# Depthwise-convolution module on one core: tap seeds in PSUM, the products of a tile in strict order, fillers in the middle of a block, and another division of the layer norm's additions

## The chip, the cores and the metric

The kernel runs on one core of one Trainium2 chip. The metric is the device time of that core in microseconds (us). A run of this kernel takes 2839.5 us (the median of three, from 2835.58 to 2844.86).

## What is computed

One inference step of a two-layer decoder for 1040 prompt columns (1024 tokens and 16 learned ones) and 32 sample columns. The change lies in the convolution module of layer 0, and in the cache work that runs in its shadow:

```
def conv_module(x, prefix, w_pw1, b_pw1, w_dw, b_dw, ln_g, ln_b, w_pw2, b_pw2):
    a, g = jnp.split(x @ w_pw1 + b_pw1, 2, axis=-1)
    u = a * jax.nn.sigmoid(g)
    y, tail = causal_dwconv(u, prefix, w_dw)          # 31 taps for each of 1024 channels
    y = jax.nn.silu(layer_norm(y + b_dw, ln_g, ln_b))
    return y @ w_pw2 + b_pw2, tail
```

The cache work is a key norm: for each of 128 cached pages the latents are multiplied by w_uk (16 heads of 64 columns), and the sum of squares of each head is kept. Layer 1 needs these sums much later.

## The kernel before

Activations lie with channels on the 128 partitions and 1074 columns (T0) along the free axis, in eight tiles of channels (KD). Each fp32 factor is split into a rounded high part and a low remainder (`split`: the high part by ScalarE, the difference by VectorE, or by GpSimd where `self.help` is set), and a product is three matmuls (`wh`, `wl` are weights, `xh`, `xl` activations).

The convolution module has four stages. First, the input's RMS norm. Second, a loop over eight tiles c: two products (value `a` and gate `g`, PSUM tiles `g`) in three thirds of 358 columns each, with 48 matmuls to a third (line 395), then `glu`: ScalarE's sigmoid (`sg`, line 378) and VectorE's product into `u` (line 379). `u` holds even and odd columns apart. Then `conv31` makes 31 taps out of three shorter filters on the even part, the odd part and their sum `fb` (line 477): `p0` with 16 taps, `p1` with 15 and `p2` with 16. ScalarE writes the first tap of each (the seed, line 481) into SBUF, and VectorE adds the others one by one in a PSUM accumulator `a` (line 488); the instruction for tap 1 reads the seed. GpSimd multiplies the ends of the filters (`ra`, line 484) and the sample columns (`p`, line 502), which VectorE sums (lines 486 and 504). ScalarE copies the state columns into `us` (lines 407, 408). Loop tiles overlap: the products of tile c run beside the taps of tile c-1.

Third, the layer norm: TensorE sums the eight tiles with a matrix of ones (line 529), VectorE subtracts the mean (line 537), ScalarE squares (543), VectorE and GpSimd add the squares (546, 549, 551), TensorE sums them over channels (287), VectorE takes the inverse root, copies it out to rows (`rx`, 264), TensorE transposes these (266) and ScalarE copies them to `rstd` (268); then each tile is scaled (426), goes through silu (428) and is split. Fourth, the second product with `pw2` (line 171; the first two of its eight tiles of outputs run side by side), and the residual (448).

The cache work is a Python generator: each `next(self.fill)` writes one group, three matmuls of 512 columns (line 603, here called a filler) and its sums of squares. By its place among the eight of a page group, the sums go to ScalarE alone (one 512-column group is eight squares of 64 columns with an accumulator, line 615), to a square (606) with a reduction by VectorE (611), or with halvings by GpSimd ahead of that (610). The constants say after how many matmuls a filler is written, and which places go to which engine: there are 256 in all, 16 and 30 ahead of the loop, 24 in each of tiles 1 to 7, then 12 and 11 among the matmuls of the mean (`FILL1`, `FILL0`), 15 behind them (`FILL2`) and 4 behind the splits (`NLN`). That uses up all 256.

The order on each engine is that of a scheduler which follows priorities and its own model of time; inside `with self.manual()` TensorE keeps the order written.

## Time and profile before

| | |
|---|---|
| median of three runs | 2839.5 us |
| profiled execution | 2836.05 us, of which the span is 2834.3 us |
| granted TensorE clock, mean | 0.966 of full speed |
| loop over tiles 1 to 6 | 129 to 396 us, 44.5 us a tile |
| last tile's convolution and mean | 403 to 455 us |
| layer norm up to the first matmul of the second product | 455 to 495 us |
| second product | 495 to 604 us |

Busy time on an engine says how long instructions ran there, not how long it held others up. On TensorE the rows overlap a little, since one matmul begins before the row of the last has ended. Stretches below are cut by hand at the places where the loop repeats.

### The profile page before, as it was taken

Reading aid. Unit: us, or ns where it says so; the run is one execution under the profiler, and the core shown is the slowest. Engines: PE = TensorE matmul, PEld = TensorE weight load, DVE = VectorE, ACT = ScalarE, POOL = GpSimd, SP = SyncE. Lnnn points to the kernel's source line nnn. Section 1 sums busy time; section 2 is a strip of 40 time slices with the busy share of each in tenths; the row PEclk is TensorE's granted clock in tenths of the full one; section 3 lists DMA queues with packets and bytes.
Section 4 is the critical chain, followed back from the end, with each engine's and each line's share of the span. In section 5 each row is a group of like instructions: output and inputs, shape, how many; then the busy total and the mean of one; then the engine's idle time right before and its main releaser. Section 6 shows DMA issues by size and latency. Waiting matters only on the chain.

```text
span 2834.3 us, 47489 instructions
## 1 busy us (share of the span) xinstructions
PE 2675.1 (94%) x16916; PEld 2456.8 (87%) x16916; DVE 1911.5 (67%) x3521; ACT 1380.9 (49%) x4074; POOL 665.5 (23%) x923
## 2 busy tenths in 40 slices
PE   7999986999999999999799999988999999999999
PEld 5888864999999999999667676656999999999999
DVE  8899997569888874234776767565358777766131
ACT  6778778435554553023555564555335544544010
POOL 1457542005333330001201212100005333321000
PEclk9999997999999999999889999978999999999999
DMA  4111110412322236122100001257502222227122
GB/s 136 55 39 57 40 48 20 153 47 76 101 80 91 85 115 225 40 93 90 37 10 26 23 16 42 73 168 225 183 33 76 72 86 78 79 86 257 45 85 74
DMA packets 127778, 238.30 MB, mean 84 GB/s; under 512 B 39779, under 2 KB 81141, under 8 KB 127413
## 3 DMA queue, kind: packets, MB, share of 16 engines
q1 hardware_dynamic: 103828, 200.82, 22.1%
q0 software_dynamic: 9600, 32.36, 3.1%
q10 hardware_dynamic: 14112, 2.09, 0.4%
q8 instruction: 133, 2.18, 0.3%
q14 instruction: 105, 0.85, 0.1%
HBM read 183.90 MB, written 51.31 MB: 83 GB/s over the span
## 4 chain that ended last, share of the span: by engine, by line
PE 80%; DVE 7%; ACT 6%; DMA 2%; issue 2%; SPq 2%; POOL 0%; ACTq 0%; DVEq 0%
PE ps L742 29%; PE ps L171 22%; PE v L1280 5%; PE pk L603 4%; PE ps L791 3%; PE g L395 3%; PE p L147 2%; DVE a L488 2%; PE ps L193 2%; ACT qq L615 2%; PE ps L960 1%; PE p L1290 1%; PE s L1250 1%; PE p L1292 1%; PE p L1293 1%
## 5 line engine op out<-in xcount | busy, mean ns | idle before, releaser
L135 ACT ACTIVATE wh<-raw 128x512 fp32r<-128x512 f32 (+2 forms) x256 | 191.3, 750 | 566.3 <-PE ps L171 360.0
L136 DVE TENSOR_TENSOR wl<-raw,wh 128x512 fp32r<-128x512 f32 (+2 forms) x244 | 201.1, 828 | 104.9 <-ACT wh L135 102.8
L888 DVE TENSOR_TENSOR x<-ps,x 128x1074 f32<-128x1074 f32 (+1 forms) x48 | 60.9, 1270 | 289.5 <-PE ps L171 289.4
L712 DVE SCALAR_TENSOR_TENSOR c<-ub,c,c 128x1040 f32<-128x1040 f32 (+1 forms) x176 | 225.2, 1312 | 30.1 <-ACT c L709 29.3
L615 ACT ACTIVATE qq<-pk 128x64 f32<-128x64 f32 x936 | 198.2, 248 | 76.8 <-PE pk L603 76.2
L615 ACT ACTIVATION_READ_ACCUMULATOR qq<-pk 128x1 f32 x936 | 194.3, 232 | 0.1
L1280 PE MATMUL v<-pf,vf 128*128 128x512 f32 (+4 forms) x448 | 180.2, 486 | 11.8 <-ACT pf L1297 11.5
L707 POOL COPY sb<-ub 128x32 f32<-128x32 f32 x88 | 88.4, 1006 | 398.1 <-DVE ub L753 359.6
L610 POOL TENSOR_TENSOR sq<-sq 128x256 f32<-128x256 f32 x198 | 130.1, 659 | 181.7 <-ACT sq L606 174.4
L603 PE MATMUL pk<-ukh,ch 128*128 128x512 f32 x256 | 115.2, 451 | 47.2 <-ACT qq L615 17.1
L1297 ACT ACTIVATE pf<-p 128x512 f32<-128x512 f32 (+4 forms) x224 | 99.5, 450 | 122.9 <-DVE p L1295 102.2
L171 PE MATMUL ps<-xh,wh 128*128 128x358 f32 (+1 forms) x672 | 147.8, 328 | 2.6 <-DVE x L888 1.6
L171 PE MATMUL ps<-xh,wl 128*128 128x358 f32 (+1 forms) x672 | 147.3, 327 | 0.4 <-DVE wl L136 0.4
L171 PE MATMUL ps<-al,wh 128*128 128x358 f32 (+1 forms) x672 | 147.2, 327 | 0.0
L171 PE MATMUL ps<-xl,wh 128*128 128x358 f32 (+1 forms) x672 | 146.8, 326 | 0.0
L171 PE MATMUL ps<-ah,wl 128*128 128x358 f32 (+1 forms) x672 | 146.5, 326 | 0.0
L171 PE MATMUL ps<-ah,wh 128*128 128x358 f32 (+1 forms) x672 | 146.2, 326 | 0.0
L488 DVE SCALAR_TENSOR_TENSOR a<-u,c,a 128x512 f32<-128x512 f32 x200 | 137.8, 742 | 0.0
L709 ACT ACTIVATE c<-ub,c 128x1074 f32<-128x1074 f32 (+1 forms) x88 | 101.3, 1185 | 67.3 <-DVE ub L753 53.1
L395 PE MATMUL g<-xh,wh 128*128 128x358 f32 x336 | 111.1, 331 | 18.0 <-DVE u L379 16.2
L171 PEld LDWEIGHTS ps<-xh,wh 128*128 128x128 f32 x672 | 116.2, 190 | 4.8 <-ACT ah L135 2.2
L135 ACT ACTIVATE wh<-s 128x512 fp32r<-128x512 f32 x120 | 75.5, 630 | 87.8 <-PE ps L742 81.2
(585 smaller groups left out, 9116.2 us busy)
## 6 DMA issues: line engine op xcount, KB each, us to landing
raw<-wup SPq DMA_DIRECT2D x88, 512.0 KB, 3.5
pg<-ctn SPq DMA_DIRECT2D x128, 192.0 KB, 2.6
raw<-wdn SPq DMA_DIRECT2D x32, 448.0 KB, 3.4
raw<-pw SPq DMA_DIRECT2D x24, 512.0 KB, 3.7
d_a<-c POOLq DMA_DIRECT2D x22, 537.0 KB, 3.5
raw<-d_a SPq DMA_DIRECT2D x22, 537.0 KB, 4.9
d_a<-c POOLq DMA_DIRECT2D x22, 531.0 KB, 3.1
raw<-d_a SPq DMA_DIRECT2D x22, 531.0 KB, 5.5
```

The costliest lines, as they stand in the source:

```text
L135: return (nc.scalar.activation(h, src, AF.Copy), (eng or nc.vector).tensor_tensor(out=l, in0=src, in1=h.bitcast(F32), op=ALU.subtract))
L136: (eng or nc.vector).tensor_tensor(out=l, in0=src, in1=h.bitcast(F32), op=ALU.subtract))
L171: nc.tensor.matmul(p[:, c, :ch], s[:, k * 128:(k + 1) * 128], m[k][:, off + c * ch:off + (c + 1) * ch], start=k == 0 and i == 0, stop=k == ...
L395: nc.tensor.matmul(p[:, 0], x[:, k * 128:(k + 1) * 128], m[k][:, t * ch:t * ch + ch], start=k == 0 and i == 0, stop=k == KD - 1 and i == 2)
L488: nc.vector.scalar_tensor_tensor(out=p[:, :ND] if j == n - 1 else acc, in0=x[:, j:j + ND], scalar=w[:, j:j + 1], in1=p[:, :ND] if j == 1 e ...
L603: nc.tensor.matmul(ps, s[:, j, :], m[:, 512 * c:512 * c + 512], start=i == 0, stop=i == 2)
L610: nc.gpsimd.tensor_tensor(out=v[:, :, :n], in0=v[:, :, :n], in1=v[:, :, n:2 * n], op=ALU.add)
L615: nc.scalar.activation(q, ps[:, 64 * h:64 * h + 64], AF.Square, accum_out=ss[:, p, 8 * c + h:8 * c + h + 1])
L709: x = nc.scalar.activation(c, ub, AF.Copy, scale=wd[:, t, 2:3])
L712: nc.vector.scalar_tensor_tensor(out=c[:, 2:pe], in0=ub[:, tap:tap + pe - 2], scalar=wd[:, t, tap:tap + 1], in1=c[:, 2:pe], op0=ALU.mult, ...
L742: nc.tensor.matmul(ps, w[:, s], m[:, lo:hi], start=first and k == 0 and i == 0, stop=k == KD // 2 - 1 and i == 2, skip_group_check=True)
L1280: nc.tensor.matmul(o[:, at_:], vf[:m, b, c], p[:m, :512 - at_], start=b == 0, stop=last)
```

## The change

Seven edits. (1) The seeds of `p0` and `p1` are written by ScalarE into the PSUM accumulator, so that tap 1 reads PSUM; the order of the two filters is turned, and `p2`, whose seed stays in SBUF, uses the accumulator of `p1`. (2) GpSimd's products `ra` and `p` wait for the addition `fb` (`after`). (3) The state copies go from ScalarE to GpSimd. (4) Each third's matmuls stand behind all of the third before (`self.wedge`), and a filler is written after three matmuls of each six. (5) `self.help` stays on in the last tile and through the mean, so that GpSimd makes the differences of cache latents there. (6) Among the matmuls of the mean there are 12 and 9 fillers, whose odd places go to GpSimd alone (it halves 64 to 1). None stand behind them in the layer norm; the 21 that are left are written into the second product, 8 into the first two tiles of outputs (`EVERY3`), the others one after each nine matmuls (`EVERY2`), with the sums on VectorE. (7) The squares are added in two heaps, 0 to 2 on GpSimd and 3 to 7 on VectorE, and TensorE sums both heaps in one accumulation (`add_rows`).

```diff
-FILL0 = 11
+FILL0 = 9
 FILL1 = 2
-FILL2 = 15
-NLN = 4
+FILL2 = 0
+NLN = 0
+EVERY3 = 18
...
-ONPL0 = ()
-ONPL1 = (0, 3, 6)
+ONPL0 = (1, 3, 5, 7)
+ONPL1 = range(8)
+HEADS = (0, 3)
...
+    def after(self, late, early):
+        why = mybir.DependencyInfo(mybir.DependencyClass.Sync, mybir.DependencyReason.DATA)
+        self.tc.add_manual_dep(late.ins, early.ins.name, why, reason="order")
...
+    def add_rows(self, t, qs, tn):
+        with self.manual():
+            for k, q in enumerate(qs):
+                for b in range(NB):
+                    lo = min(128 * b, tn - 128)
+                    self.nc.tensor.matmul(t[:, 2 * b:2 * b + 2], q[:, lo:lo + 128], self.ones[:, 0:2], start=k == 0 and b == 0,
+                                          stop=k == len(qs) - 1 and b == NB - 1, skip_group_check=True)
...
-                self.help = 0 < c < KD - 1
+                self.help = c > 0
...
-                                        nc.tensor.matmul(p[:, 0], x[:, k * 128:(k + 1) * 128], m[k][:, t * ch:t * ch + ch],
-                                                         start=k == 0 and i == 0, stop=k == KD - 1 and i == 2)
+                                        y = nc.tensor.matmul(p[:, 0], x[:, k * 128:(k + 1) * 128], m[k][:, t * ch:t * ch + ch],
+                                                             start=k == 0 and i == 0, stop=k == KD - 1 and i == 2)
+                                        self.follow(y, self.wedge)
+                                        self.wedge = []
                                         cnt += 1
-                                        if EVERY and cnt % EVERY == 0:
+                                        if EVERY and cnt % EVERY == EVERY // 2:
                                             next(self.fill, None)
+                        self.wedge = [y]
                         glu(*ps, t)
...
-                    nc.scalar.activation(us[:, 0:30].rearrange("p (b e) -> p b e", e=2), u[:, :, 520:535].rearrange("p e b -> p b e"), AF.Copy)
+                    nc.gpsimd.tensor_copy(us[:, 0:30].rearrange("p (b e) -> p b e", e=2), u[:, :, 520:535].rearrange("p e b -> p b e"))
...
-            self.on_dve, self.on_pool = ONLN, ONPL1
             self.groups(NLN)
             self.on_dve, self.on_pool = range(8), ONPL2
...
-                ahead = self.gemms(ahead, hh, ll, 0, T0, EVERY2)
+                ahead = self.gemms(ahead, hh, ll, 0, T0, EVERY3)
...
-        nc.vector.tensor_tensor(out=s, in0=u[:, 1, 0:535], in1=u[:, 0, 1:536], op=ALU.add)
-        def taps(p, x, w, n, name):
+        first = nc.vector.tensor_tensor(out=s, in0=u[:, 1, 0:535], in1=u[:, 0, 1:536], op=ALU.add)
+        def taps(p, x, w, n, name, seed=True):
             m = p.shape[1]
             acc = self.pa.tile([128, 512], F32, name=name)[:, :ND]
-            nc.scalar.activation(p[:, :ND], x[:, 0:ND], AF.Copy, scale=w[:, 0:1])
+            to = acc if seed else p[:, :ND]
+            nc.scalar.activation(to, x[:, 0:ND], AF.Copy, scale=w[:, 0:1])
...
-                                               in1=p[:, :ND] if j == 1 else acc, op0=ALU.mult, op1=ALU.add)
+                                               in1=to if j == 1 else acc, op0=ALU.mult, op1=ALU.add)
...
-        for _ in zip_longest(taps(p0, u[:, 0], w31[:, c, 0::2], 16, "a0"), taps(p1, u[:, 1], w31[:, c, 1::2], 15, "a1")):
+        for _ in zip_longest(taps(p1, u[:, 1], w31[:, c, 1::2], 15, "a1"), taps(p0, u[:, 0], w31[:, c, 0::2], 16, "a0")):
             pass
-        for _ in taps(p2, s, wsum[:, c], 16, "a0"):
+        for _ in taps(p2, s, wsum[:, c], 16, "a1", False):
...
-        self.on_dve = ONLN0
-        self.on_pool = ONPL0
+        self.on_dve, self.on_pool, self.halve = (), ONPL0, 1
...
+        sums = self.pp.tile([128, 3, 512], F32, name="ps")
+        t = sums[:, 2, 400:400 + 2 * NB]
...
+            qs = []
             for k in range(KD):
-                if k == 0:
-                    self.sq_add(sq, ys[k], 0, T0)
-                    continue
                 q = self.xpool(k).tile([128, self.tw], F32R, name=f"xl{k}").bitcast(F32)
                 nc.scalar.activation(q, ys[k], AF.Square)
-                if k in ONPOOL:
...
+                if k in HEADS:
+                    qs.append(q)
                 else:
-                    nc.vector.tensor_tensor(out=sq[:, :T0], in0=sq[:, :T0], in1=q, op=ALU.add)
-                if k == ADDAT:
-                    nc.vector.tensor_tensor(out=sq[:, :T0], in0=sq[:, :T0], in1=odd, op=ALU.add)
+                    (nc.gpsimd if len(qs) == 1 else nc.vector).tensor_tensor(out=qs[-1], in0=qs[-1], in1=q, op=ALU.add)
+            self.add_rows(t, qs, T0)
         self.groups(FILL2)
```

Three places show how the instructions move.

VectorE at the border of two tiles, before: `u` of the last third, the end of the old tile, and the start of the new one (`a_3389` and `a_3395` are the new tile's accumulators, `fa` holds the seeds).

```order
L379 SCALAR_TENSOR_TENSOR u<-g,c_58,sg 128x179x2
L488 SCALAR_TENSOR_TENSOR fb<-fb,wsum,a_2674 128x512
L498 TENSOR_TENSOR x_2631<-fb,fa 128x520
L409 MEMSET u 128x1
L477 TENSOR_TENSOR fb<-u 128x535
L486 TENSOR_REDUCE fa<-ra_3397 128x8
L488 SCALAR_TENSOR_TENSOR a_3389<-u,c_58,fa 128x512
L488 SCALAR_TENSOR_TENSOR a_3395<-u,c_58,fa 128x512
L488 SCALAR_TENSOR_TENSOR a_3389<-u,c_58,a_3389 128x512
L488 SCALAR_TENSOR_TENSOR a_3395<-u,c_58,a_3395 128x512
```

The same place with the change (`a_3392` and `a_3398` are the new tile's accumulators).

```order
L507 SCALAR_TENSOR_TENSOR fb<-fb,wsum,a_2677 128x512
L517 TENSOR_TENSOR x_2634<-fb,fa 128x520
L393 SCALAR_TENSOR_TENSOR u<-g,c_58,sg 128x179x2
L507 SCALAR_TENSOR_TENSOR a_3392<-u,c_58,a_3392 128x512
L507 SCALAR_TENSOR_TENSOR a_3398<-u,c_58,a_3398 128x512
L507 SCALAR_TENSOR_TENSOR a_3392<-u,c_58,a_3392 128x512
L427 MEMSET u 128x1
L626 TENSOR_REDUCE ss<-sq 128x8
L507 SCALAR_TENSOR_TENSOR a_3398<-u,c_58,a_3398 128x512
L495 TENSOR_TENSOR fb<-u 128x535
L507 SCALAR_TENSOR_TENSOR a_3392<-u,c_58,a_3392 128x512
```

The old tile now ends ahead of `u`, the first taps stand right behind `u`, the addition `fb` comes after four of them, and the reductions of `ra` after that.

GpSimd at the same border, before: from the last difference of weights to the first reuse of the squares.

```order
L136 TENSOR_TENSOR wl<-raw,wh 128x1024
L484 TENSOR_TENSOR ra_2643<-u,c_58 128x8x15
L610 TENSOR_TENSOR sq<-sq 128x8x32
L502 TENSOR_TENSOR p<-us,c_58 128x992
L484 TENSOR_TENSOR ra_2637<-u,c_58 128x144
L610 TENSOR_TENSOR sq<-sq 128x8x16
L136 TENSOR_TENSOR cl<-ct,ch 128x512
```

The same place with the change.

```order
L134 TENSOR_TENSOR wl<-raw,wh 128x1024
L624 TENSOR_TENSOR sq<-sq 128x8x32
L425 COPY us<-u 128x30
L426 COPY us<-u 128x32
L624 TENSOR_TENSOR sq<-sq 128x8x16
L134 TENSOR_TENSOR cl<-ct,ch 128x512
L624 TENSOR_TENSOR sq<-sq 128x8x32
L624 TENSOR_TENSOR sq<-sq 128x8x16
L503 TENSOR_TENSOR ra_2640<-u,c_58 128x8x15
L503 TENSOR_TENSOR ra_2646<-u,c_58 128x144
L521 TENSOR_TENSOR p<-us,c_58 128x992
```

Two copies and a difference `cl` (the latter stood behind the products before) now stand between `u` and the products.

VectorE in the layer norm, before: from the last mean subtraction to the inverse root (`sq` is the heap, `xl` are squares, `cl` and `ss` belong to fillers).

```order
L537 SCALAR_TENSOR_TENSOR x_6401<-ps,x_6401 128x1074
L611 TENSOR_REDUCE ss<-sq 128x8
L549 TENSOR_TENSOR sq<-sq,xl_7129 128x1074
L136 TENSOR_TENSOR cl<-ct,ch 128x512
L549 TENSOR_TENSOR sq<-sq,xl_7135 128x1074
L549 TENSOR_TENSOR sq<-sq,xl_7141 128x1074
L611 TENSOR_REDUCE ss<-sq 128x8
L549 TENSOR_TENSOR sq<-sq,xl_7144 128x1074
L551 TENSOR_TENSOR sq<-sq,xl_7127 128x1074
L611 TENSOR_REDUCE ss<-sq 128x8 x2
L251 TENSOR_SCALAR nr_v<-ps 128x9
```

The same place with the change.

```order
L554 SCALAR_TENSOR_TENSOR x_6404<-ps,x_6404 128x1074
L562 TENSOR_TENSOR xl_7016<-xl_7016,xl_7018 128x1074
L562 TENSOR_TENSOR xl_7016<-xl_7016,xl_7021 128x1074
L562 TENSOR_TENSOR xl_7016<-xl_7016,xl_7024 128x1074
L562 TENSOR_TENSOR xl_7016<-xl_7016,xl_7027 128x1074
L253 TENSOR_SCALAR nr_v<-ps 128x9
```

The fillers' rows are gone from between the additions, and four additions are left.

## Rows read from the trace of the kernel before

**Rows 1.** The page: its first line, and busy time, share of the span and number of instructions of each engine over the whole span.

```profile
span 2834.3 us, 47489 instructions
...
PE 2675.1 (94%) x16916; PEld 2456.8 (87%) x16916; DVE 1911.5 (67%) x3521; ACT 1380.9 (49%) x4074; POOL 665.5 (23%) x923
```

**Rows 2.** Busy time by stretch. Columns: the stretch, its length, busy time (and number of instructions) of PE, PEld, DVE, ACT and POOL, then the granted TensorE clock, the DMA share and GB/s. One tile in the middle of the loop, the last tile's convolution, the layer norm, and the first of the second product.

```profile
218.00:262.50 44.50, 41.31 (x218) 37.03 (x217) 43.01 (x71) 33.97 (x218) 28.94 (x34) 1.00 0.17 48
410.00:455.00 45.00, 33.73 (x103) 20.00 (x101) 36.96 (x57) 39.20 (x358) 0.60 (x2) 0.89 0.08 25
455.00:495.00 40.00, 24.86 (x77) 15.19 (x75) 29.51 (x39) 30.29 (x156) 15.42 (x14) 0.68 0.05 14
495.00:500.00 5.00, 5.00 (x16) 4.71 (x17) 5.00 (x5) 5.00 (x10) 0.00 (x0) 0.50 0.00 0
```

**Rows 3.** Waits from 129 to 396 us, which are six of the eight tiles. Columns: who waited for whom, us in total, times, longest.

```profile
PE g L395 <- DVE u L379: 16.2, 6, 3.0
...
DVE u L379 <- ACT sg L378: 5.1, 6, 1.2
```

**Rows 4.** VectorE's groups of instructions in the same six tiles. Columns: line, engine, operation, output and inputs with shapes, count, busy us, mean ns, idle time ahead of them.

```profile
L488 DVE SCALAR_TENSOR_TENSOR a<-u,c,a 128x512 f32<-128x512 f32 x150 | 103.8, 741 | 0.0
...
L488 DVE SCALAR_TENSOR_TENSOR a<-u,c,fa 128x512 f32<-128x512 f32 x12 | 26.6, 2259 | 0.0
```

**Rows 5.** VectorE in order of time, in tile 0, in a middle tile (with one row of GpSimd, POOL), and in the last tile. Columns: start, us (of all xN together), line, operation, output and inputs, count, and in brackets the idle time ahead and what ended it.

```profile
87.92 2.59 DVE L477 TENSOR_TENSOR fb<-u 128x535 f32<-128x535 f32 x1
...
226.09 0.84 DVE L477 TENSOR_TENSOR fb<-u 128x535 f32<-128x535 f32 x1
...
227.03 4.40 DVE L488 SCALAR_TENSOR_TENSOR a<-u,c,fa 128x512 f32<-128x512 f32 x2
...
227.48 3.40 POOL L502 TENSOR_TENSOR p<-us,c 128x992 f32<-128x992 f32 x1
...
405.36 2.69 DVE L477 TENSOR_TENSOR fb<-u 128x535 f32<-128x535 f32 x1
...
413.18 1.41 DVE L488 SCALAR_TENSOR_TENSOR a<-u,c,fa 128x512 f32<-128x512 f32 x2
...
430.92 0.69 DVE L136 TENSOR_TENSOR cl<-ct,ch 128x512 fp32r<-128x512 f32 x1 [2.56 <-ACT ch L135]
...
445.19 0.69 DVE L136 TENSOR_TENSOR cl<-ct,ch 128x512 fp32r<-128x512 f32 x1 [1.56 <-ACT ch L135]
```

**Rows 6.** GpSimd's groups in the six tiles, shapes apart (columns as in the group of VectorE).

```profile
L610 POOL TENSOR_TENSOR sq<-sq 128x256 f32<-128x256 f32 x71 | 56.8, 800 | 59.4 <-ACT sq L606 59.2
...
L610 POOL TENSOR_TENSOR sq<-sq 128x128 f32<-128x128 f32 x72 | 33.9, 471 | 5.2
...
L136 POOL TENSOR_TENSOR cl<-ct,ch 128x512 fp32r<-128x512 f32 x15 | 19.4, 1292 | 27.3 <-ACT ch L135 27.3
```

**Rows 7.** ScalarE: the two tap seeds of a tile, 80 to 400 us.

```profile
L481 ACT ACTIVATE fa<-u,c 128x512 f32<-128x512 f32 x14 | 9.4, 724 | 0.8 <-DVE u L409 0.3
```

**Rows 8.** GpSimd over the whole span: the two nearest forms to a small strided copy.

```profile
L707 POOL COPY sb<-ub 128x32 f32<-128x32 f32 x88 | 88.4, 1006 | 398.1 <-DVE ub L753 359.6 <-ACT ub L800 38.4
...
L1107 POOL COPY rnew<-rrk 64x4 f32<-64x4 f32 x4 | 0.8, 210 | 23.4 <-DVE rrk L256 23.4
```

**Rows 9.** The chain that ended last, in order of time (start, us, what): a block of six products and a filler in a tile, then from the last row of the layer norm into the second product.

```profile
243.20 0.69 PE pk L603 x3
243.88 0.99 PE g L395 x6
...
488.54 0.32 ACT rstd L268
...
492.76 1.17 ACT x L428
...
493.93 0.99 ACT xh L135
...
494.97 1.26 PE ps L171 x3
...
496.23 1.28 PE pk L603 x3
...
507.95 0.70 PE pk L603 x3
```

**Rows 10.** VectorE in order of time through the layer norm (columns as in the earlier timeline).

```profile
451.32 0.70 DVE L498 TENSOR_TENSOR x<-fb,fa 128x520 f32<-128x520 f32 x1
...
455.25 9.56 DVE L537 SCALAR_TENSOR_TENSOR x<-ps,x 128x1074 f32<-128x1074 f32 x8 [3.23 <-PE ps L529]
...
474.79 1.42 DVE L551 TENSOR_TENSOR sq<-sq,xl 128x1074 f32<-128x1074 f32 x1
...
480.30 0.17 DVE L251 TENSOR_SCALAR nr_v<-ps 128x9 f32<-128x9 f32 x1 [3.31 <-PE ps L287]
...
482.55 1.47 DVE L264 COPY rx<-r 128x384 f32<-128x384 f32 x3
...
488.89 3.65 DVE L426 TENSOR_TENSOR x<-x,rstd 128x1074 f32<-128x1074 f32 x3 [0.52 <-ACT rstd L268]
```

**Rows 11.** One addition of a row of squares: on VectorE outside the layer norm, and on GpSimd in it.

```profile
L279 DVE TENSOR_TENSOR sq<-sq,q 128x1074 f32<-128x1074 f32 x12 | 15.6, 1300 | 6.1 <-ACT q L278 5.9
...
L546 POOL TENSOR_TENSOR xl<-xl,xl 128x1074 f32<-128x1074 f32 x2 | 5.4, 2704 | 3.2 <-ACT xl L543 3.2
```

More of the change, by code (lines that the diff above doesn't have):

```diff
@@ L266, in spread @@
                 nc.tensor.transpose(ps[:, c, b * 128:(b + 1) * 128], rx[:, 3 * c + b, :], self.cst("ident"))
-            w = min(384, tn - 384 * c)
+            w, n = min(384, 128 * (NB - 1) - 384 * c), min(0, tn - 384 * c - 384)
             nc.scalar.activation(out[:, 384 * c:384 * c + w], ps[:, c, :w], AF.Copy)
+            if n:
+                nc.scalar.activation(out[:, 384 * c + w:tn], ps[:, c, w - n:384], AF.Copy)
     def sq_add(self, sq, x, k, tn):
@@ L272, in sq_add @@
         if k == 0:
-            if sq.shape[1] > T0:
-                nc.gpsimd.memset(sq[:, tn:], 0.0)
             nc.scalar.activation(sq[:, :tn], x, AF.Square)
@@ L289, in token_rstd, with rows_rstd @@
         return r9, ps
-    def rows_rstd(self, sq, tn):
-        r9, ps = self.token_rstd(self.sp, [sq[:, 128 * b:128 * (b + 1)] for b in range(NB)])
+    def add_rows(self, t, qs, tn):
[5 more added lines that the diff above has]
+                                          stop=k == len(qs) - 1 and b == NB - 1, skip_group_check=True)
+    def rows_rstd(self, t, ps, tn):
+        r9 = self.sp.tile([128, NB], F32, name="r9")
+        self.rsqrt(self.sp, r9, [(ALL, t[:, 0:2 * NB:2], 1.0 / D)], [128, NB])
         rstd = self.rp.tile([128, T0], F32, name="rstd")
@@ L346, in conv_phase @@
             with self.tc.high_priority(PRIO):
+                ps = self.pp.tile([128, 3, 512], F32, name="ps")
+                t = ps[:, 2, 400:400 + 2 * NB]
                 sq = self.tp.tile([128, 1152], F32, name="sq", tag="c")
@@ L501, in conv31 @@
         win = bass.AP(v.tensor, v.offset, [list(v.ap[0]), [1, NS], [8, 31]])
-        nc.gpsimd.tensor_tensor(out=p, in0=win, in1=w31[:, c:c + 1].broadcast_to([128, NS, 31]), op=ALU.mult)
+        self.after(nc.gpsimd.tensor_tensor(out=p, in0=win, in1=w31[:, c:c + 1].broadcast_to([128, NS, 31]), op=ALU.mult), first)
         t = self.sp.tile([128, NS], F32, name="s")
@@ L530, in layer_norm @@
                 self.groups(FILL1 if k < KD - 2 else FILL0 if k < KD - 1 else 0)
-        self.on_dve = ONLN
         self.on_pool = ONPL1
-        sq = self.tp.tile([128, 1152], F32, name="sq", tag="c")
-        odd = None
+        sums = self.pp.tile([128, 3, 512], F32, name="ps")
+        t = sums[:, 2, 400:400 + 2 * NB]
         with self.tc.high_priority(PRIO):
@@ L602, in cache_norms @@
                     for i, (s, m) in enumerate(((ch, self.ukh), (cl, self.ukh), (ch, self.ukl))):
-                        nc.tensor.matmul(ps, s[:, j, :], m[:, 512 * c:512 * c + 512], start=i == 0, stop=i == 2)
+                        x = nc.tensor.matmul(ps, s[:, j, :], m[:, 512 * c:512 * c + 512], start=i == 0, stop=i == 2)
+                    self.pks.append(x)
                     if 2 * j + c in self.on_dve or 2 * j + c in self.on_pool:
@@ L607, in cache_norms @@
                         v, n = q.rearrange("p (a b) -> p a b", b=64), 64
-                        while 2 * j + c in self.on_pool and n > HALVE:
+                        while 2 * j + c in self.on_pool and n > self.halve:
                             n //= 2
-                            nc.gpsimd.tensor_tensor(out=v[:, :, :n], in0=v[:, :, :n], in1=v[:, :, n:2 * n], op=ALU.add)
-                        nc.vector.tensor_reduce(out=ss[:, p, 8 * c:8 * c + 8], in_=v[:, :, :n], op=ALU.add, axis=AX.X)
+                            to = v[:, :, :n] if n > 1 else ss[:, p, 8 * c:8 * c + 8].rearrange("p (a b) -> p a b", b=1)
+                            nc.gpsimd.tensor_tensor(out=to, in0=v[:, :, :n], in1=v[:, :, n:2 * n], op=ALU.add)
+                        if n > 1:
+                            nc.vector.tensor_reduce(out=ss[:, p, 8 * c:8 * c + 8], in_=v[:, :, :n], op=ALU.add, axis=AX.X)
                     else:
```

22 lines of the change are left out of this document (9 added, 13 removed).

## The prediction, as it went on record

> **What bounds the kernel now.** I read the page first: TensorE is busy for 94% of the span, VectorE for 67%, GpSimd for 23% [rows 1]. An average says little here, so I went to the busy time by stretch, for the three stages that the change touches [rows 2]. In a middle tile of the loop, which takes 44.5 us, VectorE is busy for 43.0 us and TensorE for 41.3 us; both are nearly full. The waits show who leads: TensorE stood 16.2 us for VectorE's `u` in six tiles, once a tile, and VectorE only 5.1 us for the sigmoid [rows 3]. So the loop goes at VectorE's pace. TensorE could do better: a block of six products takes 0.99 us and its filler 0.69 us [rows 9], and 24 such pairs make 40.3 us a tile.
>
> In the last tile's convolution no products are left, and VectorE (37 of 45 us) and ScalarE (39 us, nearly all squares for fillers) alternate; GpSimd does almost nothing there (0.6 us) [rows 2]. Two of VectorE's idle times are a remainder `cl` that waits for ScalarE [rows 5]. In the layer norm the timeline of VectorE shows one long chain with fillers between its links [rows 10]. The second product is TensorE's alone.
>
> **The first taps.** The reader is to see one line of VectorE's groups: 150 ordinary taps take 741 ns each, but the 12 that read the seed take 2259 ns [rows 4]. In the last tile two such taps together take 1.41 us, in a middle tile 4.40 us [rows 5]. The shape is the same; what differs is that GpSimd works on its long product `p` (3.40 us [rows 5]) beside the slow ones and the seed is a second SBUF operand, while an ordinary tap reads its accumulator from PSUM. With the seed in PSUM I take 0.741 us: 12 x (2.259 - 0.741) = 18.2 us off VectorE in tiles 1 to 6. The Trainium skill gives this a mechanism ("SBUF — State Buffer", section "Who interferes with whom"): a VectorE instruction with two SBUF inputs and a GpSimd instruction that reads SBUF exclude each other for their whole length, and one with at most one SBUF input is left alone. By that rule the 18.2 us are gained whole; if the slowness were in the instruction itself, nothing.
>
> The change adds two costs. The accumulator of `p1` is now the one in which the old `p2` has just ended, and the first taps stand directly behind `u`, which the seed reads. So VectorE waits for one seed, 0.72 us [rows 7], about 0.8 with the handover: 4.8 us in six tiles. Bounds: 0 where other work covers it, 1.95 us a tile where both seeds (1.45 us) and some of ScalarE's squares (0.5 us, an estimate) come first. Queued behind that wait are all the taps, and for them `u` of the next third. Second, the addition `fb` moves three microseconds later, behind the copies and a remainder `cl` on GpSimd. It takes 0.84 us beside short work and 2.59 or 2.69 us beside `p` [rows 5]. `p` now waits for it, so I take half of a `cl` (1.29 us [rows 6]): 3.9 us for six tiles; bounds 0 and 6 x 1.85 = 11 us.
>
> The strict order puts the start of each third behind the last, so the bank that it needs has been free for some ten microseconds; TensorE's 16.2 us of waiting go, and with them VectorE's 5.1 us for late sigmoids. Sum: -18.2 - 5.1 + 4.8 + 3.9 = **-14.6 us**, 42.1 us a tile, still above TensorE's 40.3. Bounds: -23.3, and +5 (no 5.1, 12 and 11 paid).
>
> The state copies cost GpSimd between 0.21 and 1.0 us each [rows 8]; its 15 idle microseconds a tile [rows 2] hide them, and the samples' sums that wait for them are read far later. Without cover they would delay `p` by up to 2 us. ScalarE's saving is hidden too. In tile 0, `fb` drops from 2.59 us [rows 5]; less the copies, **-1.2 us** (0 to -1.8).
>
> **The last tile.** `fb` falls by 1.85 us, three `cl` rows of 0.68 us leave VectorE, and with them the waits of 2.56 and 1.56 us [rows 5]; some 0.8 us of short waits go as well: **-8.8 us**. GpSimd takes this over: about eleven halving chains of 0.80 + 0.47 us and four smaller steps (0.75 us together if the two rows [rows 6] are continued in a straight line), 2.0 us each, with three `cl` and the products some 31 us. VectorE has 38 us of work then, so it stays cover. Bounds: -10 and, with GpSimd late, +8 (below).
>
> **The layer norm**, link by link [rows 10]. The mean: VectorE waited 3.23 us behind the last tap, since a filler stood between; six matmuls need 2.0 us: -1.2. Eight subtractions, 9.56 us: same. Additions: from 464.8 to 476.2 us, 11.4 us; now four of 1.30 us [rows 11]: -6.2. Sums: 4.0 us, same; those of the first heap lie ahead. The root to the first scaling: 482.55 to 488.89 us; now three copies (1.47 us), a set of transposes and three or four copies of 0.32 us [rows 9]: 2.7 us, -3.6. First scaling to the first matmul: 6.1 us; now 1.22 + two silus of 1.17 + a split of 0.99 us [rows 9] and handovers, 4.65 us: -1.4. Together **-12.4 us**.
>
> A rule speaks against the additions. What the rows show is that an addition on GpSimd takes 2.70 us in this stage [rows 11], and that VectorE's became slower beside it. The same section of the skill would have such pairs run one after another, since both read two SBUF operands. Here it bites only if GpSimd is late: its two additions need the squares of tiles 1 and 2, ready while VectorE still subtracts with one operand in PSUM. If they collide, the stage keeps 5.4 us.
>
> **The second product.** 21 fillers at 0.69 us, 14.5 us, now stand where nothing covers them; three that stood there before (1.28, 0.69 and 0.70 us [rows 9]) are among those counted. **+11.8 us**. The granted clock in the first 5 us was 0.50, the lower of its levels (1.2 GHz), behind a sparse layer norm [rows 2]. I take that to be the same.
>
> **Sum:** -14.6 - 1.2 - 8.8 - 12.4 + 11.8 = -25.2 us. The profiled execution, 2836.05 us (span 2834.3 and 1.75 around it), would come to 2810.9. It lies 3.45 us under the median of the runs shown; from the median, 2839.5, I get **2814 us**. Behind the convolution module a few instructions of the attention stage change places; I price that at 0, with 4 us either way as an estimate, since its work is the same.
>
> **The rivals.** *The lock moves:* the seeds and the additions still meet GpSimd, with its new copies and chains; `fb` pays 1.85 us a tile and the seeds 1.95, and the layer norm loses 5.4. That is -25.2 + 7.2 + 6.9 + 5.4, about -6 at worst and -15 halfway: 2824. For it: `fb` at 2.59. Against: the tail of the tile before shows additions beside short GpSimd work at their normal length. *The change doesn't do it:* the first taps are slow for another reason, and stay at 2.26 us: -25.2 + 18.2 = -7, 2832. Against it stand the quick pairs in the last tile. *TensorE's pace:* seeds and `fb` come covered, tiles at 40.3 to 41 us: 10 us more, 2804. *Slower, GpSimd becomes the bound* of the last tile: were each small step as slow as the copies of 1.006 us [rows 8], a chain would take 5.3 us, eleven of them 58 and all of its work 67 us, 29 us beyond VectorE's 38. That is 4 us more than the whole gain: some 2843. It decides from about 4.9 us a chain on. Against: the same halvings took 0.80 and 0.47 us in the loop.
>
> **How the numbers follow.** Forecast 0.57 (2806 to 2822), TensorE's pace 0.12, the lock 0.16, no effect on the taps 0.08, GpSimd 0.07. A difference of under 0.3%, 8.5 us, can't be told from none here. Faster: 0.57 + 0.12 + 0.16 and a part of the others, 0.87; same 0.08; slower 0.05. From 2799 (TensorE's pace with the attention's 4 us) to 2831 (the lock) no more than 2 in 10 is left out.
>
> **What would show it.** Right: first taps at about 0.74 us in tiles 1 to 6; the line of TensorE waiting for `u` gone; tiles of 42 us; a gap of 0.8 us ahead of each first tap with ScalarE's seed as releaser; four additions of 1.3 us in a row; some 30 us from the last tap to the second product; that product 12 us longer. Wrong: first taps still above 2 us, `fb` above 1.5 us, VectorE waiting for GpSimd in the last tile, or a lower clock far into the second product.

## The result, and the profile after

The change makes the kernel faster: 2807.4 us (median of four runs, 2805.8 to 2814.1) against 2841.2 (2835.6 to 2844.9), a ratio of 0.9887 with a 95% interval of 0.9863 to 0.9911. The profiled execution took 2814.05 us, the slowest of the four; that of the kernel before, 2836.05 us, lies 5.2 us under its median. So the two traces differ by 22.0 us only, the medians by 33.9. Its page, the first two lines and then four stretches (a middle tile, the last tile, the layer norm, the first 5 us of the second product); they answer to [rows 1, 2]:

```profile
span 2812.3 us, 47232 instructions
...
PE 2666.1 (95%) x16934; PEld 2455.0 (87%) x16934; DVE 1892.0 (67%) x3526; ACT 1356.0 (48%) x3730; POOL 663.6 (24%) x988
...
218.00:260.60 42.60, 41.99 (x218) 36.95 (x218) 40.05 (x71) 33.37 (x216) 29.00 (x36) 1.00 0.17 51
390.00:428.00 38.00, 31.55 (x106) 20.85 (x107) 36.89 (x57) 28.30 (x197) 30.51 (x66) 0.92 0.11 32
428.00:461.00 33.00, 12.58 (x52) 10.21 (x50) 21.64 (x30) 14.21 (x20) 5.71 (x6) 0.58 0.10 34
461.00:466.00 5.00, 4.88 (x20) 4.37 (x21) 5.00 (x5) 4.97 (x5) 0.00 (x0) 0.68 0.00 0
```

A middle tile takes 42.6 us where it took 44.5; TensorE is busy for 42.0 of them, VectorE for 40.1. The waits of the loop (129 to 385 us; total, times, longest; they answer to [rows 3]):

```profile
DVE a L507 <- ACT a L500: 6.0, 6, 1.0
...
PE pk L615 <- ACT sq L619: 3.3, 8, 0.5
DVE u L393 <- ACT sg L392: 3.3, 6, 1.2
```

VectorE's groups there, which answer to [rows 4]:

```profile
L507 DVE SCALAR_TENSOR_TENSOR a<-u,c,a 128x512 f32<-128x512 f32 x162 | 113.5, 747 | 6.0 <-ACT a L500 6.0
...
L495 DVE TENSOR_TENSOR fb<-u 128x535 f32<-128x535 f32 x6 | 4.4, 736 | 0.0
```

And the shares of the chain through the loop:

```profile
by line: PE g L409 42.0%; PE pk L615 35.7%; ACT qq L630 5.6%; DMA raw<-pw 5.1%; POOL wl L134 3.7%; issue 3.2%; ACT sq L619 1.9%; ACT wh L133 1.7%; ACT sg L392 1.2%; ACTq L630 0.1%
```

All 162 taps of `u` on a seed or an accumulator take 747 ns; the row with 2259 ns is gone, and with it TensorE's wait for `u`. In its place VectorE waits 1.0 us a tile for the seed. The layer norm on VectorE, which answers to [rows 10]:

```profile
426.93 0.70 DVE L517 TENSOR_TENSOR x<-fb,fa 128x520 f32<-128x520 f32 x1
429.80 9.56 DVE L554 SCALAR_TENSOR_TENSOR x<-ps,x 128x1074 f32<-128x1074 f32 x8 [2.17 <-PE ps L547]
439.27 5.42 DVE L562 TENSOR_TENSOR xl<-xl,xl 128x1074 f32<-128x1074 f32 x4
448.79 0.17 DVE L253 TENSOR_SCALAR nr_v<-ps 128x9 f32<-128x9 f32 x1 [4.09 <-PE ps L298]
...
451.03 1.47 DVE L266 COPY rx<-r 128x384 f32<-128x384 f32 x3
456.06 3.65 DVE L444 TENSOR_TENSOR x<-x,rstd 128x1074 f32<-128x1074 f32 x3 [3.56 <-ACT rstd L272]
460.94 1.28 DVE L134 TENSOR_TENSOR xl<-x,xh 128x1074 fp32r<-128x1074 f32 x1 [1.22 <-ACT xh L133]
```

From the end of the last tap to the second product's first matmul it is 33.3 us now (427.63 to 460.89), 42.95 before (452.02 to 494.97). That product and what closes it then take 118.3 us to the feed-forward's first matmul (579.17), 107.2 before (602.21): 23.0 us gained at that point. Only 22.0 are left at the end. One reason is a transfer that came late in this execution. First the instruction of VectorE that reads it, then TensorE's wait behind it:

```profile
735.34 0.29 DVE L253 TENSOR_SCALAR nk<-nk 128x256 f32<-128x256 f32 x1 [2.62 <-DMA nk<-d_ss]
...
747.37 0.46 PE L757 MATMUL ps<-t3h,wh 128*128 128x268 f32 x1 [2.11 <-ACT u L765]
```

### The profile page after: what moved, and what is told of

Same layout as the page of the kernel before. It is cut to its first block, busy times and chain, and to the rows that moved or that the text cites. A ratio compares the mean times of both kernels' runs of the same rounds, so it can differ in the third digit from the quotient of the medians.

```text
span 2812.3 us, 47232 instructions
## 1 busy us (share of the span) xinstructions
PE 2666.1 (95%) x16934; PEld 2455.0 (87%) x16934; DVE 1892.0 (67%) x3526; ACT 1356.0 (48%) x3730; POOL 663.6 (24%) x988
## 4 chain that ended last, share of the span: by engine, by line
PE 83%; DVE 6%; ACT 3%; DMA 2%; issue 2%; SPq 2%; POOL 0%; ACTq 0%; DVEq 0%; POOLq 0%
PE ps L757 29%; PE ps L173 23%; PE pk L615 5%; PE g L409 4%; PE v L1295 4%; PE ps L806 3%; PE p L149 2%; PE ps L195 2%; PE ps L975 1%; PE p L1305 1%; PE s L1265 1%; PE p L1308 1%; PE p L1307 1%; DVE a L507 1%; PE ps L149 1%
## 5 line engine op out<-in xcount | busy, mean ns | idle before, releaser
L630 ACT ACTIVATE qq<-pk 128x64 f32<-128x64 f32 x760 | 163.8, 243 | 75.4 <-PE pk L615 75.4
L722 POOL COPY sb<-ub 128x32 f32<-128x32 f32 x88 | 68.4, 779 | 415.9 <-DVE ub L768 369.7
L624 POOL TENSOR_TENSOR sq<-sq 128x256 f32<-128x256 f32 (+3 forms) x234 | 141.6, 609 | 104.8 <-ACT sq L619 96.4
L630 ACT ACTIVATION_READ_ACCUMULATOR qq<-pk 128x1 f32 x760 | 159.5, 228 | 0.2
L507 DVE SCALAR_TENSOR_TENSOR a<-u,c,a 128x512 f32<-128x512 f32 x216 | 151.1, 748 | 6.0 <-ACT a L500 6.0
L619 ACT ACTIVATE sq<-pk 128x512 f32<-128x512 f32 x161 | 97.7, 612 | 46.7 <-PE pk L615 40.9
```

Source lines behind the costliest of these rows:

```text
L507: nc.vector.scalar_tensor_tensor(out=p[:, :ND] if j == n - 1 else acc, in0=x[:, j:j + ND], scalar=w[:, j:j + 1], in1=to if j == 1 else acc ...
L624: nc.gpsimd.tensor_tensor(out=to, in0=v[:, :, :n], in1=v[:, :, n:2 * n], op=ALU.add)
L630: nc.scalar.activation(q, ps[:, 64 * h:64 * h + 64], AF.Square, accum_out=ss[:, p, 8 * c + h:8 * c + h + 1])
```

## The experiments

Each is the changed kernel with one edit, unless said otherwise, timed in five rounds beside the kernel before. Two readings of each trace are steadier than the totals: the loop with the last tile (start of the first to start of the last `x<-fb,fa`, each tile's last convolution instruction) and the start of the feed-forward's first matmul on the chain. The four traces whose loop and last tile are those of the change (change, a0, e5, f2) give 295.2 to 295.7 us for the first. Both readings for the kernel before, the change and f3: the row of `x` (shortest, median and longest in ns, first and last start), then the matmul on the chain.

```profile
L498 DVE TENSOR_TENSOR x<-fb,fa x8: 695/1082/1092, 131.9 to 451.3; 128x520 f32<-128x520 f32 x8
L517 DVE TENSOR_TENSOR x<-fb,fa x8: 686/702/703, 131.2 to 426.9; 128x520 f32<-128x520 f32 x8
L503 DVE TENSOR_TENSOR x<-fb,fa x8: 697/827/1275, 130.7 to 428.8; 128x520 f32<-128x520 f32 x8
...
602.21 1.51 PE ps L791 x10
579.17 1.51 PE ps L806 x10
576.85 1.51 PE ps L796 x10
```

| run | us, median | ratio to before, 95% | loop and last tile | feed-forward starts |
|---|---|---|---|---|
| before | 2841 | 1 | 319.4 | 602.2 |
| change | 2807.4 | 0.9863 to 0.9911 | 295.7 | 579.2 |
| control (a0_again) | 2811.3 | 0.9886 to 0.9915 | 295.2 | 579.1 |
| e1_seeds_sbuf | 2817.5 | 0.9909 to 0.9935 | 302.8 | 587.2 |
| e2_products_free | 2823.7 | 0.9925 to 0.9958 | 312.1 | 594.3 |
| e3_both_undone | 2823.7 | 0.9928 to 0.9954 | 308.3 | 592.1 |
| e4_fb_first | 2817.8 | 0.9902 to 0.9932 | 299.2 | 584.1 |
| e5_adds_one_engine | 2814.3 | 0.9886 to 0.9920 | 295.6 | 582.0 |
| e6_last_tile_scalar | 2814.2 | 0.9889 to 0.9923 | 295.1 | 581.1 |
| e7_copies_scalar | 2816.6 | 0.9901 to 0.9935 | 298.2 | 581.1 |
| f1_thirds_free | 2816.3 | 0.9903 to 0.9931 | 298.3 | 580.5 |
| f2_fill_norm | 2813.9 | 0.9885 to 0.9916 | 295.2 | 579.5 |
| f3_conv_alone | 2807.9 | 0.9869 to 0.9901 | 298.1 | 576.9 |
| g1_old_norm | 2810.5 | 0.9889 to 0.9920 | 295.5 | 582.4 |

**a0_again**, no edit.

> The changed kernel once more, as the control for the stages of the others. In its first profile VectorE waited 2.62 us for a row of norms read back from DRAM at 735 us, TensorE then stood for 2.11 us and ran at the lower clock behind it, and from the start of the feed-forward to the end of its long product 6.5 us of the 23.0 us gained by then were lost again. If this was that one execution's own late transfer, this profile has no such gap and its span is some 2805 us (ratio to the kernel before 0.987 to 0.989). If the changed order causes it, the gap is here again and the span is 2811 to 2813 us.

VectorE waited 1.46 us for the same row of norms, TensorE not at all. From the feed-forward's start to the attention's the control took 726 us, the first profile 732. All other traces took 725 to 729 us. So the late transfer was that execution's own, at 3 to 7 us. It explains little of the distance between runs: the control, without it, is at 2811.3 us in the median, 4 us above the change's own.

**e1_seeds_sbuf**

```diff
-            to = acc if seed else p[:, :ND]
+            to = p[:, :ND]
```

> The seeds alone go back to SBUF; the order of the thirds, the wait of GpSimd's products for fb and all else stay. Theory 1 (the recorded one: a seed in SBUF makes the first tap slow while GpSimd works): the 12 first taps of tiles 1 to 6 are back at about 2.26 us, VectorE gets 18 us more work less the 6.0 us that it now waits for seeds, and the kernel is 10 to 15 us slower than the control. Theory 2 (GpSimd's long product p was the neighbour, and it now stands behind fb): the taps take 0.74 to 1.3 us beside the shorter GpSimd work that is left, and the kernel is within 4 us of the control. Theory 3 (TensorE leads the loop now: in the changed kernel's chain of the loop TensorE has 78%, VectorE's taps nothing): the taps may be slow, but VectorE has about 2.4 us of slack in a tile of 42.6 us, so that of 3 us a tile only about 1 us shows, 4 to 8 us in all.

VectorE's groups in the loop, first taps, the last instruction `x`, and `fb`:

```profile
L507 DVE SCALAR_TENSOR_TENSOR a<-u,c,fa 128x512 f32<-128x512 f32 x12 | 14.5, 1250 | 0.3 <-ACT fa L500 0.3
...
L517 DVE TENSOR_TENSOR x<-fb,fa 128x520 f32<-128x520 f32 x6 | 9.8, 1628 | 0.1
...
L495 DVE TENSOR_TENSOR fb<-u 128x535 f32<-128x535 f32 x6 | 5.3, 886 | 0.2
```

One wait of VectorE there:

```profile
DVE u L427 <- POOL us L426: 6.4, 6, 2.0
```

The first taps take 1.25 us, not 2.26: with `p` behind `fb`, only shorter GpSimd work is left beside them. That is theory 2's number, but the kernel loses 6 us in all and 7.6 up to the last tap. Part of it is order: `x` now stands behind `u`, beside GpSimd's `wl`, and pays 0.9 us a tile, and the zero that `fb` needs waits for the copies.

**e2_products_free**

```diff
-            self.after(nc.gpsimd.tensor_tensor(out=r, ...), first)
+            nc.gpsimd.tensor_tensor(out=r, ...)
...
-        self.after(nc.gpsimd.tensor_tensor(out=p, in0=win, ...), first)
+        nc.gpsimd.tensor_tensor(out=p, in0=win, ...)
```

> The waits of GpSimd's three small products and of p for fb are taken away; the seeds stay in PSUM. Theory 1 (the recorded one: fb, with two SBUF operands, is held up by p where p comes first): fb takes 2.6 us again in the tiles where p starts ahead of it, 1.85 us more in each of six or seven tiles, 11 to 13 us of VectorE's time; the first taps stay at 0.74 us. If VectorE leads the loop the kernel is 8 to 13 us slower than the control, if TensorE leads (theory 3) 0 to 5 us slower. Rival: fb stands ahead of p in any case, stays at 0.74 us, and the kernel is within 2 us of the control.

VectorE's groups in the loop:

```profile
L507 DVE SCALAR_TENSOR_TENSOR a<-u,c,a 128x512 f32<-128x512 f32 x162 | 112.4, 744 | 5.8 <-ACT a L500 5.8
...
L495 DVE TENSOR_TENSOR fb<-u 128x535 f32<-128x535 f32 x6 | 16.4, 2730 | 0.0
```

The timeline of one `fb` and of GpSimd's `p` beside it:

```profile
272.99 2.41 DVE L495 TENSOR_TENSOR fb<-u 128x535 f32<-128x535 f32 x1
...
271.88 2.95 POOL L521 TENSOR_TENSOR p<-us,c 128x992 f32<-128x992 f32 x1
```

In the control, where `p` comes behind `fb`, four taps beside it:

```profile
269.53 2.72 DVE L507 SCALAR_TENSOR_TENSOR a<-u,c,a 128x512 f32<-128x512 f32 x4
...
269.02 3.01 POOL L521 TENSOR_TENSOR p<-us,c 128x992 f32<-128x992 f32 x1
```

Theory 1: with the seed in PSUM the taps keep their length with `p` right beside them, and the stall has moved to `fb`. It began at 272.99, `p` ended at 274.83, `fb` at 275.40, 0.57 us later; alone it takes 0.71 us, so nearly all of its work lies behind `p`. `fb` takes 12.0 us more in the six tiles, and the median is 12.4 us higher. That the two agree so well is chance: in the trace the loop with the last tile is 16.9 us longer, and the six runs lie between 2815.6 and 2831.3 us, wider than those of any other run. VectorE's time still counts, about in full.

**e3_both_undone**, both edits at once.

> Both at once: seeds in SBUF and the products free, as before the change; the order of the thirds and the fillers in mid-block stay. Theory 1: first taps about 2.26 us and fb 0.8 to 2.6 us, a tile of 44 to 45 us, 15 to 20 us slower than the control: the whole gain of the loop (12.8 us up to the last tile) came from the two together. Theory 3: tiles of 43 to 43.5 us, 4 to 8 us slower, since the order of the thirds alone takes most of TensorE's waits for u away.

VectorE's first taps in the loop:

```profile
L507 DVE SCALAR_TENSOR_TENSOR a<-u,c,fa 128x512 f32<-128x512 f32 x12 | 26.1, 2220 | 0.6 <-ACT fa L500 0.6
```

TensorE's one wait there, 3.4 us in the control:

```profile
PE pk L615 <- ACT sq L619: 13.5, 12, 1.7
```

The slow first taps of before [rows 4] are back: 12 us slower, a little under theory 1's 15 to 20. TensorE doesn't wait for `u` here, since the order of the thirds stayed; it waits for ScalarE's squares instead, and the time is lost all the same. Three runs together show what a half is worth: e3, with neither, and e2, with the seeds in PSUM alone, are both 12 us slower than the control, e1, with the lead of `fb` alone, 6 us. The turned order of the two filters is in all three, so it isn't what pays by itself.

**f3_conv_alone**: the kernel before with the new function for the taps, and nothing else.

```diff
-            nc.scalar.activation(p[:, :ND], x[:, 0:ND], AF.Copy, scale=w[:, 0:1])
+            to = acc if seed else p[:, :ND]
+            nc.scalar.activation(to, x[:, 0:ND], AF.Copy, scale=w[:, 0:1])
...
-            nc.gpsimd.tensor_tensor(out=r, ...)
+            self.after(nc.gpsimd.tensor_tensor(out=r, ...), first)
...
-        for _ in zip_longest(taps(p0, ..., "a0"), taps(p1, ..., "a1")):
+        for _ in zip_longest(taps(p1, ..., "a1"), taps(p0, ..., "a0")):
```

> The kernel before the change with the new tap function alone: seeds in PSUM, the products behind fb, p1 ahead of p0. All else is as before: thirds in loose order, fillers at a block's end, copies on ScalarE, the old layer norm. Theory 1 (the pair of seeds and fb's lead is worth its 10 us by itself): the first taps take 0.74 us, fb 0.7 to 0.9 us, tiles of 42.5 to 43.5 us, the layer norm and the second product as before, the kernel 8 to 12 us faster than the one before (ratio 0.996 to 0.997). Rival (TensorE, loosely ordered, can't use what VectorE gains): the taps are quick, TensorE still waits for u, and the kernel is within 5 us of the one before.

VectorE's taps and `fb` in the loop:

```profile
L493 DVE SCALAR_TENSOR_TENSOR a<-u,c,a 128x512 f32<-128x512 f32 x167 | 116.5, 745 | 0.0
...
L481 DVE TENSOR_TENSOR fb<-u 128x535 f32<-128x535 f32 x7 | 6.3, 897 | 0.1
```

The fillers alone (tile `pk`) in its second product, by windows:

```profile
471.70:576.85 105.15, 0.86 (x3) 0.54 (x3) 4.45 (x29) 0.97 0.36 124
```

And in that of the change:

```profile
460.80:579.17 118.37, 17.87 (x63) 11.32 (x63) 12.45 (x21) 0.97 0.32 110
```

Both theories were too small. The tap function alone gains 25.4 us up to the feed-forward (602.2 to 576.9) and 31 in the total, as much as the whole change. It leaves one filler in the second product, the change 21: 13 us there, against 9 us in the norm (42.3 us from the last tap here, 33.3 in the change). That it beats the change isn't shown: the intervals overlap. From one `x` to the next its four middle tiles take 41.7 to 42.4 us, less than the change's 42.6 to 42.8; the other parts of the change pay in the tile ahead of the last (45.7 us, 51.5 here).

**f1_thirds_free**

```diff
-                        self.wedge = [y]
+                        self.wedge = []
-                self.wedge = self.wedge if c < KD - 1 else []
+                self.wedge = []
```

> The changed kernel without the order of the thirds: a third's first product needn't follow the last of the third before; fillers in mid-block and all else stay. With seeds and products both undone the tiles still took 44.2 us against 44.6 before the change, so the order seems to carry little in the middle tiles, but that run still gained 9 of the loop's 20 us (from the end of tile 0's convolution to that of tile 6: 270.0 us there, 279.4 before, 259.8 in the control), in the first tile of the loop and the one ahead of the last. Recorded theory (the order takes TensorE's waits for u away): those waits return, up to 16 us of TensorE's time, and that stretch takes 266 to 272 us. Rival (the waits were only the face of VectorE being late, which the seeds and fb repair): the stretch stays at 260 to 262 us, and the kernel within 2 us of the control.

TensorE's wait for `u`, in the loop:

```profile
PE g L409 <- DVE u L393: 3.6, 3, 1.2
```

3.6 us came back, not 16, and the loop with the last tile is 3.1 us longer. The tap function alone, with loose thirds, shows no such wait. So the order is worth some 3 us here; the 16 us were the face of VectorE being late.

**e4_fb_first**

```diff
-                nc.vector.scalar_tensor_tensor(...)
-                yield
+                y = nc.vector.scalar_tensor_tensor(...)
+                yield self.follow(y, [first] if j == 1 and seed else [])
```

> One dependency more in the changed kernel: the first two taps stand behind the addition fb in VectorE's queue. In the control VectorE waits 1.05 us for the first seed, right behind u, in each of tiles 1 to 6 (6.1 us), and fb (0.71 us) comes three taps later. Theory 1 (VectorE leads the loop as the prediction had it): fb covers 0.7 us of the wait, the tile falls from 42.6 to 41.9 us and the kernel by 3 to 4.5 us. Theory 2 (TensorE and ScalarE lead the loop now: they have 79% and 14% of its chain in the control): the tile stays at 42.6 us, the kernel within 1.5 us, and VectorE is idle elsewhere. Rival: fb can't run ahead, since the zero that it reads is written only when GpSimd's copies have read that place (in the run with the seeds in SBUF VectorE waited 0.97 us for those copies); then the wait changes its name, and the kernel stands within 1.5 us or is up to 2 us slower.

VectorE at the head of a middle tile:

```profile
264.85 0.85 DVE L393 SCALAR_TENSOR_TENSOR u<-g,c,sg 128x358 f32<-128x358 f32 x1 [0.36 <-ACT sg L392]
265.53 1.65 DVE L517 TENSOR_TENSOR x<-fb,fa 128x520 f32<-128x520 f32 x1
267.47 0.06 DVE L427 MEMSET u<- 128x1 f32 x1 [0.29 <-POOL us L426]
267.57 1.12 DVE L495 TENSOR_TENSOR fb<-u 128x535 f32<-128x535 f32 x1
```

Slower by 4.0 us up to the last tap and 6.5 in all, which no theory had. (TensorE's share of the chain in the control is 71%, not 79% as the expectation says.) The wait for the seed is gone, but the scheduler put `x` behind `u`, where GpSimd's `wl` runs, and `fb` meets GpSimd's halving: 0.95 and 0.4 us more of instructions with two SBUF operands.

**e7_copies_scalar**

```diff
-                    nc.gpsimd.tensor_copy(us[:, 0:30]..., u[:, :, 520:535]...)
+                    nc.scalar.activation(us[:, 0:30]..., u[:, :, 520:535]..., AF.Copy)
```

and the same for the second copy.

> The two state copies of each tile are ScalarE's again. Recorded theory: they are hidden on either engine, and the tile stays at 42.6 us, the kernel within 1.5 us of the control. Rival: ScalarE's squares free the fillers' banks, for which TensorE waits (2.9 us in five tiles, and 7.5% of the loop's chain is ScalarE's squares), and the copies stand ahead of the seeds: two copies of 0.2 to 0.3 us a tile, 2 to 4 us slower in all.

VectorE's waits for the sigmoid (3.3 us in the control) and for the copies (none there), and TensorE's for the squares (3.4 us there):

```profile
DVE u L393 <- ACT sg L392: 7.2, 6, 1.2
...
DVE u L427 <- ACT us L426: 3.2, 6, 0.5
...
PE pk L615 <- ACT sq L619: 4.9, 13, 0.5
```

The rival's price: 3.0 us longer up to the last tap (the total, 5 us more, overlaps with the control's). VectorE's waits only change places, since the control's 6.1 us for the seeds are gone; TensorE's wait for the squares, the rival's mechanism, grew by 1.5 us, and the rest isn't traced. ScalarE was not free cover.

**e5_adds_one_engine**

```diff
-HEADS = (0, 3)
+HEADS = (0,)
-                    (nc.gpsimd if len(qs) == 1 else nc.vector).tensor_tensor(...)
+                    nc.vector.tensor_tensor(...)
```

> The squares of the layer norm are added in one heap, all on VectorE; GpSimd adds none. Recorded theory: GpSimd's two additions lie beside the subtractions and cost nothing, so VectorE gets three additions of 1.36 us more than its four: the stage from the last tap to the second product goes from 33.3 to about 37.4 us. Rival (the two engines hold each other up where both read two SBUF operands): without GpSimd's additions VectorE's subtractions and additions get shorter, and the stage stands at 33 to 35 us.

The timeline of VectorE's additions in its layer norm:

```profile
438.36 9.57 DVE L562 TENSOR_TENSOR xl<-xl,xl 128x1074 f32<-128x1074 f32 x7
```

37.4 us from the last tap to the product, as the recorded theory said. Three additions of 1.37 us are what GpSimd's two save.

**e6_last_tile_scalar**

```diff
-ONPL0 = (1, 3, 5, 7)
+ONPL0 = ()
```

> In the last tile's convolution the squares of all 21 fillers go to ScalarE again, none to GpSimd; the remainders cl stay on GpSimd. A filler's eight squares with their reads take ScalarE some 1.9 us, against 0.65 us where GpSimd adds the halves: some 11 fillers make 13.5 us more, 46 us of ScalarE's work in a tile of 36.8 us. Recorded theory (GpSimd's chains are what frees the last tile): the mean's matmuls stand behind the fillers in TensorE's queue and come 6 to 10 us later. Rival (the gain came from cl, fb and the order alone): VectorE's taps never wait for a filler, and the last tap and the mean come within 2 us of the control.

VectorE's first two subtractions of the mean:

```profile
432.67 2.46 DVE L554 SCALAR_TENSOR_TENSOR x<-ps,x 128x1074 f32<-128x1074 f32 x2 [6.53 <-PE ps L547]
```

Between the two theories: the last tap comes as in the control, the mean 4.4 us later. GpSimd's chains don't quicken the convolution; they get the fillers out of the mean's way.

**f2_fill_norm**

```diff
-FILL2 = 0
+FILL2 = 6
```

> Six of the fillers that the change puts into the second product go back to the layer norm, behind its sums (6 groups there, their squares still on ScalarE and GpSimd). In the control TensorE is busy for 12.6 of the 33 us of the layer norm, at a granted clock of 0.58, and each filler costs 0.69 us where the second product starts. Theory 1 (the fillers' place is worth their TensorE time): the layer norm keeps its 33.3 us, and the second product gets shorter by 6 x 0.69 = 4.1 us, by up to 2 us more if it starts at a higher granted clock. Rival (a square of 0.65 us on ScalarE and a chain of 2.0 us on GpSimd stand between the links of the norm's chain, as in the kernel before): the norm gets 3 to 6 us longer, and nothing or less is left.

The timeline of VectorE's additions and of GpSimd's second one:

```profile
441.85 8.21 DVE L562 TENSOR_TENSOR xl<-xl,xl 128x1074 f32<-128x1074 f32 x4
...
441.97 2.45 POOL L562 TENSOR_TENSOR xl<-xl,xl 128x1074 f32<-128x1074 f32 x1
```

The chain there, with the first of the four:

```profile
441.94 3.63 DVE xl L562
```

The rival: the norm is 4.7 us longer, the product 5 shorter. Fillers' chains made GpSimd late, its addition fell beside VectorE's first, which took 3.63 us, and the four took 8.21 us instead of 5.42.

**g1_old_norm**: the loop of the change with the layer norm and the fillers of before. Of its edit against the changed kernel, the fillers:

```diff
-FILL0 = 9
+FILL0 = 11
-FILL2 = 0
-NLN = 0
+FILL2 = 15
+NLN = 4
...
-                ahead = self.gemms(ahead, hh, ll, 0, T0, EVERY3)
+                ahead = self.gemms(ahead, hh, ll, 0, T0, EVERY2)
```

> The loop of the changed kernel (tap function, order of the thirds, fillers in mid-block, copies and the last tile's remainders on GpSimd) with the old layer norm: its 21 fillers and their squares on ScalarE, the additions in one chain, the old sums. The recorded exchange: 12.4 us out of the layer norm, 11.8 us into the second product, nearly nothing left. Measured so far, from the last tap to the end of the second product: 148.7 us before the change, 150.1 in the control, 145.9 with the tap function alone. Theory 1 (the exchange gains nothing): loop as in the control (tile 42.6 us), the last tile 1 to 3 us longer for want of GpSimd's chains, norm and product together 146 to 149 us, the kernel 0 to 4 us faster than the control (ratio 0.987 to 0.990). Theory 2 (the exchange is worth what the norm's 9.7 us say): the old norm's 42 to 43 us come back and the product gives back less than 8 us, the kernel 2 to 6 us slower than the control (ratio 0.991 or more).

The timeline of VectorE, its first subtraction of the mean:

```profile
438.11 1.28 DVE L547 SCALAR_TENSOR_TENSOR x<-ps,x 128x1074 f32<-128x1074 f32 x1 [10.25 <-PE ps L539]
```

The total is the control's; the feed-forward starts 3.3 us later. The mean waits 10.25 us, because the quicker convolution now ends before ScalarE is through its fillers. Both theories hold halfway: up to the feed-forward the exchange gains some 3 us in the new loop, nothing against the old one (below). The totals, 2810.5 and 2811.3 us, don't show even that.

## Why the prediction was right

The total, 2814 us, lies 6.6 us above the measured median, and 2807.4 us is inside the range and the forecast's band. For the profiled execution the sum said 2810.9 us, and 2814.05 was measured. That this is so close is in part luck: the steps below missed by +3.0, -2.8, +2.7, -0.8 and +1.0 us, and most of it cancels. Step by step, cut where the prediction cut:

- **Tiles 0 to 6:** forecast -15.8 (14.6 and 1.2), measured -12.8 (`u` of the last tile at 390.1 instead of 402.9). The first taps fell to 0.75 us as said, and the gap ahead of them is 1.0 us, said 0.8. Tile 0's -1.2 didn't show: the last `u` of tile 1 stands at 133.1 us in both traces. Mis-sized: the sigmoid's 5.1 us, of which 3.3 stayed, and `fb`'s 3.9 us, which weren't paid (0.736 us, less than before). The rival of the moved lock was real, but needs `p` ahead of `fb`; the dependency prevents just that, as e2 shows. And the 18.2 us aren't the seeds' alone, as the sum has it: e2, with the seeds but not the lead of `fb`, is no faster than e3, with neither.
- **Who leads:** the prediction kept VectorE in the lead. In the chain TensorE and ScalarE now hold 78% and 10%, VectorE's taps nothing. But e2 passes on what it adds, so the engines stand close together. TensorE is busy for 42.0 us of a tile, not for the prediction's 40.3.
- **Why TensorE's waits go:** the prediction gave them to the order of the thirds, which is the lesser half. The order without the quick taps does remove the row (e3), but TensorE then waits 13.5 us for ScalarE's squares, and the middle tiles still take 44.0 to 45.0 us. The quick taps remove the row without the order (f3), and those tiles take 41.7 to 42.4.
- **Last tile:** -8.8 forecast, -11.6 measured (49.1 to 37.5 us). Its price list was right in kind; a halving chain takes 2.4 us on GpSimd, said 2.0. The cut flatters it: before, 9 us of the old tile's convolution still stood behind the new `u`; from the start of one `x` to the next it is 40.0 us before (411.3 to 451.3) and 36.1 now (390.8 to 426.9). GpSimd's chains held out, as forecast against the rival.
- **Layer norm:** -12.4 forecast, -9.7 measured. Mean -1.1, additions -6.0, first scaling to first matmul -1.2 were right. The failed term is the root to the scaling: 2.7 us said, 5.0 measured (451.03 to 456.06), since three sets of transposes alternate with ScalarE's copies, waiting 3.56 us.
- **Second product:** +11.8 forecast, +11.0 measured, 21 fillers. With the norm: +1.3 us, so the exchange gained nothing here, and the forecast's own two terms said -0.6.
- **Copies:** costed at nothing; e7 puts them at 3 us, in the change's favour.
- **Attention and feed-forward:** 0 forecast with 4 us either way; +1.0, made of 6 us for the late transfer and -5 from the attention on (1506.4 to 1500.9 us). The cause of the -5 stays open; the control shows -3.

What the sum didn't say is that one function carries it all. It priced the first taps at 18.2 us and more than that on the last tile and the layer norm; f3 gives the tap function 25 us by itself, and the other parts take about as much as they give. No run had both halves with the old order of the filters.

The Trainium skill's "SBUF — State Buffer", section "Who interferes with whom", says that a VectorE instruction with two SBUF inputs and a GpSimd instruction that reads SBUF shut each other out. These traces agree: e2's `fb` of 2.41 us ended 0.57 us behind `p`, while taps with one SBUF input kept 744 ns in e2, and 0.68 us each beside `p` in the control.

## What to carry to other kernels

When one shape of instruction has two prices in a trace, look at the neighbouring engine's row at the slow ones. Removing the second SBUF operand is half a repair: the next instruction with two of them takes the stall over, so give the short one the lead over the long one too (e1 and e2, a half each, lose 6 and 12 us against the control; in f3 both halves with the new tap order are worth as much as the whole change). And time the parts of a bundle singly: here moving fillers from one stage to the next looked like 10 us in the stage and was nothing in the sum against the old loop.
